# Gates beside the attention heads, branch projections over all heads behind them

## The chip, the cores and the metric

The kernel runs on one core of a Trainium2 chip. The metric is the device time of one execution in microseconds (us). Engines are named as in the profile: PE is TensorE (PEld its weight loads), DVE is VectorE, ACT is ScalarE, POOL is GpSimd, SP is SyncE. SP and POOL issue the DMA transfers that matter here. A name such as L290 is line 290 of the kernel before.

## The reference

One layer of an encoder block: 512 tokens and 16 learned meta tokens (L = 528), model width 1024, float32. Cut to what matters:

```python
xn = rmsnorm(h, norm_mix_g)
proj = xn @ w_in                      # q, k, v of 8 stick-breaking and 8 differential heads
o_sb = stick_breaking(...)            # 528 x 1024, 8 heads of 128
o_df = rmsnorm_per_head(diff_attn(...)) * (1 - lam_init)
y_sb = o_sb @ w_br_sb
y_df = o_df @ w_br_df
gates = sigmoid(xn @ w_gate + b_gate)     # two gates of width 1024
merged = gates[0] * y_sb + gates[1] * y_df
h = h + merged @ w_out
h = h + (silu(hn @ w_ffn_gate) * (hn @ w_ffn_up)) @ w_ffn_down     # hn = rmsnorm(h)
y = rmsnorm(h, norm_final_g)              # meta tokens dropped
```

## The kernel before

**Arithmetic.** Every matrix product is taken in three passes: an operand is split into a high part rounded to the matmul's format (`_h`) and a low rest (`_l`), and PE adds high·high, high·low and low·high in PSUM (`mm3`, L290 to L292). A weight tile is loaded by SP to `wst`, cast to `wh` by ACT (L78), and its rest `wl` is made by DVE (L79).

**Layout.** Activations lie transposed, channels on the 128 partitions and tokens along the line. `xT_h` and `xT_l` hold the normed input, eight tiles of 128 channels; the 16 meta tokens come first, so that the 512 tokens (`QT`) start 64 bytes into a line. A block of a projection (128 output channels, 512 tokens) is 8 input tiles x 3 passes = 24 matmuls of 128x512 into one of four PSUM banks of the pool `ps_mm`; `halves` gives it as two units of 12.

**Order of the work.** A loop runs over two branches (`br`; 0 stick-breaking, 1 differential) and eight heads each. While head `h` computes its attention (`sb_head` or `df_head`, a generator that yields between its scores, its transposes and its product with the values), the loop pops units from the list `units` between these steps: the q, k and v projections of head `h+1` (`sb_units`, `df_units`), the transposing of its v (`turn`, L532 and L539), and what `more` holds. Each popped unit also lets the background list issue one transfer or so by POOL (`tick`): the block sums of the output and down projections' weights, kept in DRAM and partly accumulated there (`ds`, `os`). A scheduler then sets the order on each engine by dependencies and priorities; PSUM evacuations have raised priority. Weights are prepared in the order of the list `stream`.

**Gates and branch projections before.** `more` holds `y_units`: when two heads are done, their outputs (`o`, a high and a low tile for two heads, in the pool `opool`) are multiplied by the two heads' rows of the branch weight. For each of 8 output tiles that is one group of 6 matmuls, a copy by ACT (L799) and a transfer of 256 KB by POOL to `y_part` in DRAM, accumulating there from the second pair on (L801, L803). Of the 16 gate blocks, two (f = 0) run in the first two stick-breaking heads, four (f = 1, 2) around the last differential head, ten in the merge.

**The last head's norm.** The norm of a differential head runs late, in the next head: `late` holds it, with two matmuls by ones (L772, L773), Ln and Exp on ACT (L774, L775), two DVE steps (L776, L777), and the split into `o_h` (ACT, L778) and `o_l` (DVE, L779). The last head's norm is popped after the loop.

**Merge before.** For each of eight channel tiles f the two y tiles are read back from DRAM (`y_back`, L1070), multiplied with the two gates (L1127, POOL for f < 6, DVE for the rest) and added (L1131); `merge_sums` makes the split operands and block sums for the output projection. The residual tile `hres` (L1138, four transfers of 512 KB by POOL) takes the tag `y_sb` of the pool `xtp`; output projection, feed-forward layer and down projection follow and are not touched.

Of the kernel before, what the change touches and what calls it, by code (L numbers as in the profile page):

```python
# [9 lines left out]
F32 = mybir.dt.float32  # L10
# [6 lines left out]
P = 128  # L17
# [24 lines left out]
def block_kernel(ctx: ExitStack, tc: tile.TileContext, x, meta, norm_mix_g, w_in, w_gate, b_gate,  # L42
# [15 lines left out]
    def mm_tile():  # L58
        return ps_mm.tile([P, 512], F32, tag="mm", name="mm")
# [23 lines left out]
    def cols(key, view, c0):  # L83
        stream.append((key, view, c0, P, 0, KT))

    def rows(key, view, c0, k0):
        stream.append((key, view, c0, 512, k0, k0 + 2))

    for h in range(NH):

        for i in (0, 1, 2) if h < SEVEN else (2, 1, 0):
            cols(("sb", h, i), w_in, i * D + h * P)
        if 0 < h < 3:
            cols(("gate", h - 1, 0), w_gate, (h - 1) * D)
        if h > 2:
            rows(("y_sb", h - 3), w_br_sb, (h + 1) % 2 * 512, (h - 3) // 2 * 2)
    for h in range(NH):
        for i in range(3):
            cols(("df", h, i), w_in, (3 + i) * D + h * P)
        if h < 3:  # L100
            rows(("y_sb", h + 5), w_br_sb, (h + 1) % 2 * 512, (h + 5) // 2 * 2)
        else:
            rows(("y_df", h - 3), w_br_df, (h + 1) % 2 * 512, (h - 3) // 2 * 2)
    rows(("y_df", 5), w_br_df, 512, 4)
    for f in range(1, 3):
        for br in range(2):
            cols(("gate", br, f), w_gate, br * D + f * P)
    for i in range(2):
        rows(("y_df", 6 + i), w_br_df, i * 512, 6)
    for f in range(3, KT):  # L110
        for br in range(2):
            cols(("gate", br, f), w_gate, br * D + f * P)
# [220 lines left out]
    y_count, y_out = [0], []  # L333

    tA = xtp.tile([P, 2, 2, 4, HL], F32R, tag="y_sb", name="tA")
    y_part = {n: [ydram.tile([P, SEQ], F32, name=f"{n}_{f}") for f in range(KT)] for n in ("y_sb", "y_df")}
    mid = ExitStack()
    opool = mid.enter_context(tc.tile_pool(name="opool", bufs=2))

# [271 lines left out]
    def sb_head(h, d, o_h, o_l):  # L611
        qh, ql = d["q"]
        kh, kl = d["k"]
        zA, zB = z_tile(), z_tile()
# [79 lines left out]

    late = []

    def df_head(h, d, o_h, o_l):
# [72 lines left out]
        def norm():  # L770
# [7 lines left out]
            nc.scalar.activation(o_h, of, AF.Copy, scale=g_sub)  # L778
            nc.vector.scalar_tensor_tensor(o_l, of, g_sub, o_h.bitcast(F32), op0=ALU.mult, op1=ALU.subtract)  # L779

        late.append(norm)


    def y_units(name, i, o):

        def unit(fs):
            wh, wl = weights((name, i))
            for f in fs:
                ps = mm_tile()
                cs = slice(f % 4 * P, (f % 4 + 1) * P)  # L790
                mm3(ps, [(wh[:, k, cs], wl[:, k, cs], o[0][:, k], o[1][:, k]) for k in range(2)])
                if y_out:
                    ys = y_out[0][:, y_count[0] % KT]
                elif y_count[0] % 2:
                    ys = ap_.tile([P, SEQ], F32, tag="ys", bufs=2, name="ys")
                else:
                    ys = gate_tile(0)
                y_count[0] += 1
                nc.scalar.copy(ys, ps)  # L799
                if i < 2:  # L800
                    nc.gpsimd.dma_start(y_part[name][f], ys)  # L801
                else:
                    nc.gpsimd.dma_start(y_part[name][f], ys, accum_op=ALU.add)  # L803

        f0 = i % 2 * 4
        return [lambda: unit((f0, f0 + 1)), lambda: unit((f0 + 2, f0 + 3))]

    def gate(br, f, dst, func):
        def evac(ps):
# [1 line left out]

        return halves(("gate", br, f), xT, QT, evac)

    g_part = [ydram.tile([P, SEQ], F32, name=f"g_{br}") for br in range(2)]

    def gate_out(br):
        g = gate_tile(0)
        first, second = gate(br, 0, g, AF.Identity)

        def rest():  # L820
            second()
            nc.gpsimd.dma_start(g_part[br], g)

        return [first, rest]

# [179 lines left out]
    order.close()  # L1005
    units[5]()
    turn()
    todo = []
    for br in range(2):
        name, head = (("y_sb", sb_head), ("y_df", df_head))[br]  # L1010
        if br:
            nc.gpsimd.memset(a_s, 0.0)
            y_out.append(xtp.tile([P, KT, SEQ], F32, tag="y_sb", name="y_out"))
        for h in range(NH):
            if (br, h) == (0, 0):
                tB["t"] = opool.tile([P, 2, 2, 4, HL], F32R, tag="y_df", name="tB", bufs=1)
                sums = sum_units()
            if (br, h) == (0, 4):
                df_constants()
            if h % 2 == 0:  # L1020
                o = [opool.tile([P, 2, SEQ], F32R, tag=t, name=t) for t in ("o_h", "o_l")]
            if h + 1 < NH:
                nd, units, turn = (sb_units, df_units)[br](h + 1)
            elif br == 0:
                nd, units, turn = df_units(0)
            else:
                units, turn = [], None
            more = todo.pop(0) if todo else []
            if br == 0 and h < 2:
                more = gate_out(h)  # L1030
            if turn is None:
                sg0 = [gate_tile(br) for br in range(2)]
                units = more + gate(0, 1, sg0[0], AF.Identity) + gate(1, 1, sg0[1], AF.Identity)
            else:
                units = units + more[0:1] + [turn] + more[1:]
# [3 lines left out]
            for n in head(h, d, o[0][:, h % 2], o[1][:, h % 2]):  # L1039
# [6 lines left out]
            if h % 2:  # L1046
                todo += [y_units(name, h - 1 + i, o) for i in range(2)]
    sg1 = [gate_tile(br) for br in range(2)]
    units = gate(0, 2, sg1[0], AF.Identity) + gate(1, 2, sg1[1], AF.Identity)
    units[0]()  # L1050
    late.pop(0)()
    for u in units[1:]:
        u()
    for units in todo:
        for u in units:
            u()
    for sg in sg0 + sg1:
        nc.scalar.activation(sg, sg, AF.Sigmoid)
    att.close()


# [13 lines left out]
    tp_ctx = ExitStack()
# [35 lines left out]
            else:  # L1111
                last_sums.append(rest)

    merge_order = [1, 2, 0, *range(3, KT)]
    ys = [y_back(f) for f in merge_order[:2]]
    for i, f in enumerate(merge_order):
        sg = (sg0, sg1)[i] if i < 2 else [gate_tile(br) for br in range(2)]
        if i + 2 < KT:
            ys.append(y_back(merge_order[i + 2]))
        for br, y in enumerate(ys[i]):  # L1120
            if f == 0:
                nc.sync.dma_start(sg[br], g_part[br])
                nc.scalar.activation(sg[br], sg[br], AF.Sigmoid)
            elif f > 2:
                for u in gate(br, f, sg[br], AF.Sigmoid):
                    u()
            (nc.gpsimd if f < 6 else nc.vector).tensor_tensor(sg[br], sg[br], y, op=ALU.mult)  # L1127
# [81 lines left out]
    def to_out(t, half, ps, op, last=False):  # L1209
        cs = slice(half * 512, (half + 1) * 512)  # L1210
        with tc.high_priority(offset=EVAC):
            nc.vector.tensor_tensor(hres[:, t, cs], hres[:, t, cs], ps, op=op)  # L1212
        if last:
            sq = mgp.tile([P, 512], F32, tag="y_sb", bufs=2, name="sq")
# [320 lines left out]
```

## Time and profile before

| | |
|---|---|
| median of 3 runs | 955.26 us (954.28 to 955.35) |
| the profiled execution | 955.27 us, span 953.5 us, granted PE clock 0.998 |
| PE busy | 940.6 us, 99% |
| DVE, ACT, POOL busy | 720.8, 592.8, 190.5 us (76, 62, 20%) |
| DMA | 158.42 MB, mean 166 GB/s |
| HBM read, written | 133.64 MB, 50.86 MB |

The span is the time from the first to the last instruction; the execution's own time has some 1.8 us around it. In a row of the timeline stand the start, the duration, engine, line, operation, output<-inputs, and in brackets the idle time before it with what ended it. Matmuls are pipelined: they start 0.227 us apart and take 0.39 us each, so the distance between starts is what counts. Start and input norm take the first 55 us, stick-breaking heads run to about 271, differential heads to 497, the last norm to 509, the merge to 573, the output projection to 616, the feed-forward layer to 841, the down projection to the end.

### The profile page before, as it was taken

How to read it: one execution, taken by the hardware profiler on the slowest of the kernel's cores; microseconds unless marked ns; L12 is line 12 of the kernel's file. 1: busy time of each engine (PE TensorE's matmuls, PEld its weight loads, DVE VectorE, ACT ScalarE, POOL GpSimd, SP SyncE). 2: the span in 40 equal slices, each digit the busy share in tenths (PEclk: the TensorE clock that was granted, in tenths of full speed). 3: DMA queues.
4: the chain of work that ended last, by engine and by line, in shares of the span. 5: the costliest groups of instructions: out<-in, count | busy, mean ns of one | idle time of the engine just before them, and what ended most of it. 6: DMA issues, size and time to landing. Idle time of an engine off the chain costs nothing.

```text
span 953.5 us, 16249 instructions
## 1 busy us (share of the span) xinstructions
PE 940.6 (99%) x6105; PEld 851.1 (89%) x6106; DVE 720.8 (76%) x1336; ACT 592.8 (62%) x1137; POOL 190.5 (20%) x212
## 2 busy tenths in 40 slices
PE   8999999999999999999999999999999999999996
PEld 5988989898999899998987888899999999988886
DVE  7978777765677666876662578899888888989875
ACT  7765676666566666666676356765555555666654
POOL 3200121222133343344513530001000000000013
PEclk9999999999999999999999999999999999999999
DMA  8525678778777879799987865527743343276642
GB/s 246 154 63 149 164 176 204 159 166 228 198 178 174 213 170 185 181 204 180 199 198 168 260 197 170 150 78 171 155 123 111 90 120 103 67 255 203 198 151 89
DMA packets 155824, 158.42 MB, mean 166 GB/s; under 512 B 6465, under 2 KB 117218, under 8 KB 155746
## 3 DMA queue, kind: packets, MB, share of 16 engines
q1 hardware_dynamic: 132690, 101.61, 35.5%
q0 software_dynamic: 22896, 55.72, 28.6%
q8 instruction: 48, 0.79, 0.3%
q14 instruction: 30, 0.25, 0.1%
q10 hardware_dynamic: 160, 0.07, 0.0%
HBM read 133.64 MB, written 50.86 MB: 193 GB/s over the span
## 4 chain that ended last, share of the span: by engine, by line
PE 90%; DVE 6%; ACT 2%; issue 1%; DMA 1%; ACTq 0%; DVEq 0%
PE mm L290 21%; PE mm L291 21%; PE mm L292 21%; PE z L290 6%; PE z L291 6%; PE z L292 6%; PE z L708 1%; PE z L707 1%; DVE wl L79 1%; PE tr L556 1%; PE tr L532 1%; PE z L556 1%; DMA slots<-in_w_ffn_down_dram 1%; PE z L584 1%; DVE hres L1212 1%
## 5 line engine op out<-in xcount | busy, mean ns | idle before, releaser
L290 PE MATMUL mm<-xT_h,wh 128*128 128x264 f32 (+2 forms) x656 | 214.5, 327 | 0.5 <-ACT xT_h L912 0.5
L291 PE MATMUL mm<-xT_l,wh 128*128 128x264 f32 (+2 forms) x656 | 213.4, 325 | 0.5
L292 PE MATMUL mm<-xT_h,wl 128*128 128x264 f32 (+2 forms) x656 | 212.5, 324 | 0.0
L79 DVE TENSOR_TENSOR wl<-wst,wh 128x1024 fp32r<-128x1024 f32 (+1 forms) x147 | 164.2, 1120 | 44.9 <-ACT wh L78 44.7
L78 ACT CAST wh<-wst 128x1024 fp32r<-128x1024 f32 (+1 forms) x147 | 141.6, 965 | 84.7 <-PE mm L291 62.5
L291 PEld LDWEIGHTS mm<-xT_l,wh 128*128 128x128 f32 x656 | 123.5, 188 | 10.1 <-DVE xT_l L913 1.3
L290 PEld LDWEIGHTS mm<-xT_h,wh 128*128 128x128 f32 x656 | 123.5, 188 | 10.0 <-ACT xT_h L912 0.9
L292 PEld LDWEIGHTS mm<-xT_h,wl 128*128 128x128 f32 x656 | 123.4, 188 | 10.0
L290 PE MATMUL mm<-hT_h,wh 128*128 128x256 f32 x304 | 85.7, 284 | 0.4 <-ACT hT_h L1169 0.4
L292 PE MATMUL mm<-hT_h,wl 128*128 128x256 f32 x304 | 86.0, 284 | 0.0
L291 PE MATMUL mm<-hT_l,wh 128*128 128x256 f32 x304 | 86.0, 283 | 0.0
L290 PEld LDWEIGHTS mm<-hT_h,wh 128*128 128x128 f32 x304 | 57.3, 189 | 0.6 <-ACT hT_h L1169 0.6
L291 PEld LDWEIGHTS mm<-hT_l,wh 128*128 128x128 f32 x304 | 57.6, 190 | 0.0
L292 PEld LDWEIGHTS mm<-hT_h,wl 128*128 128x128 f32 x304 | 57.4, 189 | 0.0
L711 DVE CUSTOM_DVE_ANT_0 pr<-z,bias 128x144 f32<-128x144 f32 (+3 forms) x64 | 30.9, 501 | 35.0 <-PE z L708 34.9
L290 PE MATMUL mm<-o_h,wh 128*128 128x512 f32 x128 | 53.2, 416 | 0.0
L1437 POOL TENSOR_TENSOR outs<-hres,gF 128x512 f32<-128x512 f32 x4 | 6.2, 1554 | 226.0 <-DVE hres L1423 217.8
L291 PE MATMUL z<-wl,da 128*128 128x512 f32 (+1 forms) x132 | 50.4, 381 | 0.3 <-DVE wl L79 0.3
L145 POOL DMA_DIRECT2D ds<-in_w_ffn_down_dram x36 | 30.1, 840 | 102.3 <-ACT wh L78 68.6
L291 PE MATMUL mm<-o_l,wh 128*128 128x512 f32 x128 | 50.1, 392 | 0.3 <-DVE o_l L779 0.3
L290 PE MATMUL z<-wh,da 128*128 128x512 f32 (+1 forms) x132 | 50.2, 381 | 0.0
L292 PE MATMUL z<-wh,da 128*128 128x512 f32 (+1 forms) x132 | 50.2, 380 | 0.0
(375 smaller groups left out, 2554.4 us busy)
## 6 DMA issues: line engine op xcount, KB each, us to landing
wst<-in_w_in_dram SPq DMA_DIRECT2D x40, 512.0 KB, 5.7
ds<-in_w_ffn_down_dram POOLq DMA_DIRECT2D x30, 512.0 KB, 6.2
wst<-in_w_ffn_gate_dram SPq DMA_DIRECT2D x22, 512.0 KB, 4.0
wsu<-in_w_ffn_up_dram SPq DMA_DIRECT2D x20, 512.0 KB, 3.8
wst<-in_w_gate_dram SPq DMA_DIRECT2D x16, 512.0 KB, 6.8
y_df<-y_out POOLq DMA_DIRECT2D x32, 256.0 KB, 7.4
slots<-ds SPq DMA_DIRECT2D x13, 512.0 KB, 3.4
os<-in_w_out_dram POOLq DMA_DIRECT2D x12, 512.0 KB, 5.4
```

Of the source, the lines that this page charges most:

```text
L78: cast["last"] = (hi_copy or nc.scalar.copy)(hi, src)
L79: (lo_eng or nc.vector).tensor_tensor(lo, src, hi.bitcast(F32), op=ALU.subtract)
L145: tc.add_manual_dep(nc.gpsimd.dma_start(dst, src, **kw).ins, cast["last"].ins.name, paced)
L290: nc.tensor.matmul(ps, lhsT=ah, rhs=bh, start=(start and i == 0), stop=False, skip_group_check=skip)
L291: nc.tensor.matmul(ps, lhsT=ah, rhs=bl, start=False, stop=False, skip_group_check=skip)
L292: nc.tensor.matmul(ps, lhsT=al, rhs=bh, start=False, stop=(stop and i == n - 1), skip_group_check=skip)
L532: nc.tensor.transpose(pt[:, j * P:(j + 1) * P], vT[:, j * P:(j + 1) * P], ident)
L556: nc.tensor.transpose(pt[:, (t - j) * P:(t - j + 1) * P], blocks(t, j * P, (j + 1) * P), ident)
L584: nc.tensor.matmul(ps.rearrange("p (t q) -> p t q", q=P)[:, :, lo_rows:P], lhsT=vf[:, 1], rhs=a_s[:, 0:4 * qn], start=False, stop=True)
L707: nc.tensor.matmul(o, lhsT=q[c][:, qs], rhs=k[c][:, 0, k0:k1], start=True, stop=False)
L708: nc.tensor.matmul(o, lhsT=q[c][:, qs], rhs=k[c][:, 1, k0:k1], start=False, stop=True)
L711: nc.vector.tensor_tensor_reduce(po, zz, bb, scale=1.0, scalar=-3.0e38, op0=ALU.add, op1=ALU.max, accum_out=mx[:, t, c:c + 1])
```

## The change

Gates move ahead: 16 gate blocks run beside the heads, two in stick-breaking heads 0 and 7, one in every other up to differential head 5. ACT adds the bias only, POOL writes each of them to its own tile `g_part` in DRAM (256 KB), and the merge reads it back (`gate_back`, SP) and takes the sigmoid in place.

Branch projections move behind: `branch` is a block of 24 matmuls over all eight heads, in two halves of four heads. The first halves of y_sb 0 and 1 run in differential head 6; their second halves and y_sb 2 and 3 in differential head 7, and ACT copies them to tiles `ys`. y_df 0 to 7 and y_sb 4 to 7 run in the merge, and DVE multiplies them by the gate straight out of PSUM. POOL multiplies the four early ones.

Head outputs are kept: `keep` writes a pair's high and low tile to DRAM (POOL, 512 KB each; four stick-breaking pairs and two differential ones), and `back` reads two pairs by SP into a tile of `xtp` whose data start 64 bytes into the line: stick-breaking heads 0 to 3 under the tag `y_sb` at differential head 4, stick-breaking heads 4 to 7 and differential heads 0 to 3 in place of `xT_h` and `xT_l` at differential head 7. The outputs of differential heads 4 to 7 stay in `opool`, unshifted.

```diff
+    gates = [(br, f) for f in range(KT) for br in range(2)]
...
-            rows(("y_sb", h - 3), w_br_sb, (h + 1) % 2 * 512, (h - 3) // 2 * 2)
+        for _ in range((0, 2)[h] if h < 2 else 1):
+            gate_cols()
...
+    for f in range(4):
+        cols(("y_sb", f), w_br_sb, f * P)
+    for f in range(KT):
+        if f > 3:
+            cols(("y_sb", f), w_br_sb, f * P)
+        cols(("y_df", f), w_br_df, f * P)
...
+        if h % 2:
+            keep(0, h // 2, o)
...
-    def y_units(name, i, o):
-
-        def unit(fs):
-            wh, wl = weights((name, i))
-            for f in fs:
-                ps = mm_tile()
-                cs = slice(f % 4 * P, (f % 4 + 1) * P)
-                mm3(ps, [(wh[:, k, cs], wl[:, k, cs], o[0][:, k], o[1][:, k]) for k in range(2)])
...
-                nc.scalar.copy(ys, ps)
-                if i < 2:
-                    nc.gpsimd.dma_start(y_part[name][f], ys)
-                else:
-                    nc.gpsimd.dma_start(y_part[name][f], ys, accum_op=ALU.add)
...
+    def keep(br, p, o):
+        for i in range(2):
+            nc.gpsimd.dma_start(o_part[br, p][:, i], o[i].bitcast(F32))
...
+    def branch(name, f, evac):
+        cell, key = {}, (name, f)
+
+        def part(k0):
+            if k0 == 0:
+                cell["ps"] = mm_tile()
+            wh, wl = weights(key)
+            mm3(cell["ps"], [(wh[:, k], wl[:, k], *head_out[name, k]) for k in range(k0, k0 + 4)], k0 == 0, k0 == 4)
+
+        def second():
+            part(4)
+            with tc.high_priority(offset=EVAC):
+                evac(cell["ps"])
+
+        return [lambda: part(0), second]
...
+    def back(tile, br, p0):
+        for p in range(p0, p0 + 2):
+            for i in range(2):
+                nc.sync.dma_start(tile[:, p - p0, i].bitcast(F32), o_part[br, p][:, i])
+            for j in range(2):
+                head_out[("y_sb", "y_df")[br], 2 * p + j] = tile[:, p - p0, 0, j], tile[:, p - p0, 1, j]
+
+    def heads_tile(tag):
+        return xtp.tile([P, NM + KT * SEQ], F32R, tag=tag, name="ob")[:, NM:].rearrange("p (a i j c) -> p a i j c", a=2, i=2, j=2)
...
+            if (br, h) == (1, NH - 2):
+                ys = [gate_tile(f % 2) for f in range(4)]
+                early = [branch("y_sb", f, lambda ps, f=f: nc.scalar.copy(ys[f], ps)) for f in range(4)]
+                units = units + [early[0][0], turn, early[1][0]]
+            elif turn is None:
+                back(heads_tile("xT_h"), 0, 2)
+                back(heads_tile("xT_l"), 1, 0)
+                units = [early[0][1], early[1][1], *early[2], *early[3]]
...
+            if (br, h) == (1, 4):
+                back(heads_tile("y_sb"), 0, 0)
...
+            if br and h > 3:
+                head_out["y_df", h] = o[0][:, h % 2], o[1][:, h % 2]
...
+    def gate_back(br, f):
+        g = gate_tile(f % 2) if br == 0 and f > 3 else mgp.tile([P, SEQ], F32, tag="y_df", name="gb", bufs=2)
+        nc.sync.dma_start(g, g_part[br, f])
+        return g
...
+        g = gb[i]
+        nc.scalar.activation(g, g, AF.Sigmoid)
...
+        if br == 0 and f < 4:
+            nc.gpsimd.tensor_tensor(ys[f], g, ys[f], op=ALU.mult)
+            continue
+        later[f] = lambda ps: nc.vector.tensor_tensor(g, ps, g, op=ALU.mult)
+        for u in ahead[f][1:] if f < 2 else branch(("y_sb", "y_df")[br], f, later[f]):
+            u()
```

Three places show how instructions move. A row has its number, the line, the operation and output<-inputs with its shape. First PE in a differential head, where v of the next head is transposed (`vT`, `v_s`) ahead of the product of the attention weights (`a_h`, `a_l`) with the values. Before:

```order
2740 L571 MATMUL tr<-ident,pr 112x64
2741 L532 MATMUL tr<-ident,vT 128x128 x4
2742 L539 MATMUL tr<-ident,v_s 128x128
2743 L290 MATMUL z<-a_h,vh 128x512
2744 L291 MATMUL z<-a_l,vh 128x512
2745 L292 MATMUL z<-a_h,vl 128x512
```

After:

```order
2788 L571 MATMUL tr<-ident,pr 112x64
2789 L532 MATMUL tr<-ident,vT 128x128 x4
2790 L290 MATMUL z<-a_h,vh 128x512
2791 L539 MATMUL tr<-ident,v_s 128x128
2792 L291 MATMUL z<-a_l,vh 128x512
2793 L292 MATMUL z<-a_h,vl 128x512
```

The transpose of `v_s` has moved behind the first matmul of the product.

Second ACT around the last head's norm (`of`, `sq`, `o_h`). Before:

```order
575 L78 CAST sqh<-sq 128x512
576 L774 ACT_TABLE_LOAD
577 L774 ACTIVATE sq<-tr,eps_c 128x512
578 L78 CAST wh<-wst 128x1024
579 L810 ACTIVATE sg<-mm,pcol 128x512
580 L775 ACT_TABLE_LOAD
581 L775 ACTIVATE sq<-sq 128x512
582 L1058 ACT_TABLE_LOAD
583 L1058 ACTIVATE sg<-sg 128x512
584 L778 ACTIVATE o_h<-of,g_sub 128x512
585 L78 CAST wh<-wst 128x1024
```

After:

```order
541 L78 CAST sqh<-sq 128x512
542 L776 ACTIVATE sq<-tr,eps_c 128x512
543 L777 ACTIVATE sq<-sq 128x512
544 L780 ACTIVATE o_h<-of,g_sub 128x512
545 L78 CAST wh<-wst 128x1024
546 L1126 ACT_TABLE_LOAD
547 L1126 ACTIVATE gb<-gb 128x512 x2
```

The gate's evacuation and sigmoid, a weight cast and three table loads have left the chain; one table load stands behind it.

Third SP's queue from the last weights of the heads' projections on (`op` are the kept head outputs in DRAM, branch and pair; `ob` the tiles they are read into). Before:

```order
46 L204 DMA wst<-in_w_in_dram 128x8x128 x3
47 L204 DMA wst<-in_w_br_df_dram 128x2x512 x2
48 L204 DMA wst<-in_w_gate_dram 128x8x128 x4
49 L204 DMA wst<-in_w_br_df_dram 128x2x512 x2
50 L204 DMA wst<-in_w_gate_dram 128x8x128
```

After:

```order
50 L204 DMA wst<-in_w_in_dram 128x8x128 x3
51 L204 DMA wst<-in_w_br_sb_dram 128x8x128 x4
52 L204 DMA wst<-in_w_br_df_dram 128x8x128 x2
53 L1014 DMA ob<-op_0_134 128x1024
54 L1014 DMA ob<-op_2_132 128x1024 x2
55 L1014 DMA ob<-op_3_133 128x1024 x2
56 L1014 DMA ob<-op_0_134 128x1024
57 L1014 DMA ob<-op_1_135 128x1024 x2
58 L204 DMA wst<-in_w_br_df_dram 128x8x128 x2
```

Eight reads of 512 KB now stand between the weights of y_df 1 and y_df 2. The first of them is a differential pair's high tile, the next four are stick-breaking heads 4 to 7.

More of the change, by code (lines that the diff above doesn't have):

```diff
@@ L87, in rows, with gate_cols @@
         stream.append((key, view, c0, 512, k0, k0 + 2))
+    gates = [(br, f) for f in range(KT) for br in range(2)]
+    gate_of = iter(gates)
+    def gate_cols():
+        br, f = next(gate_of)
+        cols(("gate", br, f), w_gate, br * D + f * P)
     for h in range(NH):
@@ L99, in block_kernel @@
             cols(("df", h, i), w_in, (3 + i) * D + h * P)
-        if h < 3:
-            rows(("y_sb", h + 5), w_br_sb, (h + 1) % 2 * 512, (h + 5) // 2 * 2)
-        else:
[L103 to L112, printed above, removed]
+        for _ in range((h < NH - 1) + (h == 0)):
+            gate_cols()
+    for f in range(4):
[4 more added lines that the diff above has]
+        cols(("y_df", f), w_br_df, f * P)
     sums_dram = ctx.enter_context(tc.tile_pool(name="sums_dram", bufs=1, space=bass.MemoryType.DRAM))
@@ L332, in block_kernel @@
     ydram = ctx.enter_context(tc.tile_pool(name="ydram", bufs=1, space=bass.MemoryType.DRAM))
-    y_count, y_out = [0], []
     tA = xtp.tile([P, 2, 2, 4, HL], F32R, tag="y_sb", name="tA")
-    y_part = {n: [ydram.tile([P, SEQ], F32, name=f"{n}_{f}") for f in range(KT)] for n in ("y_sb", "y_df")}
+    g_part = {g: ydram.tile([P, SEQ], F32, name=f"g{g[0]}_{g[1]}") for g in gates}
+    o_part = {(br, p): ydram.tile([P, 2, 2, SEQ], F32, name=f"op{br}_{p}") for br in range(2) for p in range(4 - 2 * br)}
     mid = ExitStack()
@@ L609, in sb_units, with sb_head @@
         return d, q + kv if h < SEVEN else kv[0:3] + q + kv[3:], turn
-    def sb_head(h, d, o_h, o_l):
+    def sb_head(h, d, o_h, o_l, o):
         qh, ql = d["q"]
@@ L695, in block_kernel, with df_head @@
     late = []
-    def df_head(h, d, o_h, o_l):
+    def df_head(h, d, o_h, o_l, o):
         q, k = d["q"], d["k"]
@@ L812, in gate, with gate_out @@
         return halves(("gate", br, f), xT, QT, evac)
-    g_part = [ydram.tile([P, SEQ], F32, name=f"g_{br}") for br in range(2)]
-    def gate_out(br):
+    def gate_out(br, f):
         g = gate_tile(0)
-        first, second = gate(br, 0, g, AF.Identity)
+        first, second = gate(br, f, g, AF.Identity)
         def rest():
             second()
-            nc.gpsimd.dma_start(g_part[br], g)
+            nc.gpsimd.dma_start(g_part[br, f], g)
         return [first, rest]
@@ L1007, in block_kernel @@
     turn()
-    todo = []
+    gate_of = iter(gates)
+    def back(tile, br, p0):
[6 more added lines that the diff above has]
+        return xtp.tile([P, NM + KT * SEQ], F32R, tag=tag, name="ob")[:, NM:].rearrange("p (a i j c) -> p a i j c", a=2, i=2, j=2)
     for br in range(2):
-        name, head = (("y_sb", sb_head), ("y_df", df_head))[br]
+        head = (sb_head, df_head)[br]
         if br:
             nc.gpsimd.memset(a_s, 0.0)
-            y_out.append(xtp.tile([P, KT, SEQ], F32, tag="y_sb", name="y_out"))
         for h in range(NH):
@@ L1027, in block_kernel @@
                 units, turn = [], None
[L1028 to L1033, printed above, removed]
+            if (br, h) == (1, NH - 2):
[6 more added lines that the diff above has]
+                units = [early[0][1], early[1][1], *early[2], *early[3]]
             else:
+                more = [u for _ in range(2 if (br, h) in ((0, 0), (0, NH - 1)) else 1) for u in gate_out(*next(gate_of))]
                 units = units + more[0:1] + [turn] + more[1:]
+            if (br, h) == (1, 4):
+                back(heads_tile("y_sb"), 0, 0)
             if (br, h) == (0, 0):
@@ L1045, in block_kernel @@
             d = nd
[L1046 to L1050, printed above, removed]
-    late.pop(0)()
[L1052 to L1058, printed above, removed]
+            if br and h > 3:
+                head_out["y_df", h] = o[0][:, h % 2], o[1][:, h % 2]
+    later = {}
+    ahead = [branch("y_df", f, lambda ps, f=f: later[f](ps)) for f in range(2)]
+    ahead[0][0]()
+    late.pop(0)()
+    ahead[1][0]()
     att.close()
@@ L1213, in to_out @@
         if last:
-            sq = mgp.tile([P, 512], F32, tag="y_sb", bufs=2, name="sq")
+            sq = mgp.tile([P, 512], F32, tag="y_df", bufs=2, name="sq")
             s0, s1 = ssq[t][:, 0:1], ssq[t][:, 1:2]
```

52 lines of the change are left out of this document (15 added, 37 removed).

## The prediction

> **What bounds the kernel now.** I read the page first, for which engine is full, then the waits of TensorE (PE), then the stretches of the span one by one, and last single rows at the places that the change touches. The page:
>
> ```profile
> span 953.5 us, 16249 instructions
> PE 940.6 (99%) x6105; PEld 851.1 (89%) x6106; DVE 720.8 (76%) x1336; ACT 592.8 (62%) x1137; POOL 190.5 (20%) x212
> ...
> PE 90%; DVE 6%; ACT 2%; issue 1%; DMA 1%; ACTq 0%; DVEq 0%
> ```
>
> PE is busy for 99% of the span and carries 90% of the chain that ended last. The waits of PE (engine, line, what it waited for; total us, times, longest) name what little is missing, and the stretches say where it lies (each engine's busy us and instructions, then clock, DMA share, GB/s):
>
> ```profile
> PE z L556 <- DVE a_l L559: 0.7, 1, 0.7
> ...
> 271.00:497.00 226.00, 226.00 (x1464) 205.42 (x1464) 156.35 (x403) 149.81 (x351) 86.97 (x95) 1.00 0.85 190
> 497.00:510.00 13.00, 12.66 (x54) 9.71 (x53) 5.93 (x7) 10.79 (x14) 0.00 (x0) 1.00 0.26 65
> 510.00:573.00 63.00, 63.00 (x280) 52.14 (x279) 33.87 (x51) 28.41 (x48) 27.95 (x24) 1.00 0.81 233
> ```
>
> The three stretches are the differential heads, the last head's norm and the merge. PE is busy in all of the first and the last, and short of 0.34 us in the norm, at a granted clock of 1.00. A busy PE could still be a slow one, so I took its pace from starts inside one block:
>
> ```profile
> 499.61 0.39 PE L290 MATMUL mm<-xT_h,wh 128*128 128x512 f32 x1
> ...
> 506.88 0.39 PE L292 MATMUL mm<-xT_h,wl 128*128 128x512 f32 x1
> ```
>
> There are 33 starts from the first to the last of these, so 32 steps in 7.27 us: 0.227 us for one. A block of 24 takes 5.45 us, a half block 2.73. The change keeps the matmuls that are not transposes: 16 gate blocks of 24 stay 16, and 64 branch groups of 6 become 16 blocks of 24, 384 either way. What it can win is therefore PE's overhead and stalls, and what it can lose is a new wait of PE.
>
> **The change part by part.** First what it lifts off the other engines, by the longest group of its kind:
>
> ```profile
> L799 ACT COPY y_out<-mm x40: 558/585/588, 284.2 to 519.7; 128x512 f32<-128x512 f32 x40
> ```
>
> The 64 copies out of PSUM (0.58 us each, 37 us of ACT) and their 64 transfers of 256 KB on POOL's queue go, and the 16 reads back; 16 gate writes (2 before), 16 gate reads, 12 writes and 12 reads of 512 KB for the head outputs come. But PE is busy for 226.00 of 226.00 in the differential heads: an ACT with less to do there (149.81 busy) ends nothing earlier. Worth 0; the cover is PE's own work, and it stays.
>
> *More switches.* In the differential heads the transpose of v_s (L539) leaves its place behind the four of L532 and lands behind the first matmul of the attention product. Such a transpose between matmuls is shown in the first head:
>
> ```profile
> 36.55 0.37 PE L290 MATMUL z<-kh,qh 128*128 128x264 f32 x1
> 36.75 0.28 PE L539 MATMUL tr<-ident,v_s 128*128 128x128 f32 x1
> 36.78 0.37 PE L291 MATMUL z<-kl,qh 128*128 128x264 f32 x1
> 36.99 0.28 PE L292 MATMUL z<-kh,ql 128*128 128x264 f32 x1
> ...
> 436.35 0.66 PE L532 MATMUL tr<-ident,vT 128*128 128x128 f32 x4
> 436.84 0.27 PE L539 MATMUL tr<-ident,v_s 128*128 128x128 f32 x1
> 436.87 0.48 PE L290 MATMUL z<-a_h,vh 128*128 128x512 f32 x1
> 437.19 0.39 PE L291 MATMUL z<-a_l,vh 128*128 128x512 f32 x1
> ```
>
> A step of these 264-column matmuls is 0.12 by the pace (0.227 x 264/512). The transpose makes two steps of 0.23 and 0.21, so it costs 0.20; in a row of transposes it costs 0.12 (0.49 for four). And after a row the first matmul takes 0.32 (436.87 to 437.19) where the pace is 0.23: the switch is 0.09. Once more in 7 heads (their v is turned in differential heads 0 to 6) is +0.6 us. Bounds: 0 if the row's end becomes cheaper by as much, +0.7 at 0.10.
>
> *The last norm.* Before, sigmoids of gates stand among its Ln and Exp on ACT, and each change of function loads a table:
>
> ```profile
> 499.37 0.40 PE L773 MATMUL tr<-sqh,ones_r 128*128 128x512 f32 x1
> ...
> 507.83 0.50 PE L290 MATMUL mm<-o_h,wh 128*128 128x512 f32 x1
> 508.62 0.50 PE L291 MATMUL mm<-o_l,wh 128*128 128x512 f32 x1 [0.29 <-DVE o_l L779]
> ...
> 503.30 1.28 ACT L775 ACT_TABLE_LOAD   x1
> 504.59 0.63 ACT L775 ACTIVATE sq<-sq 128x512 f32<-128x512 f32 x1
> ...
> 505.26 0.75 DVE L776 SCALAR_TENSOR_TENSOR sq<-tr,var_max,sq 128x512 f32<-128x512 f32 x1 [1.30 <-ACT sq L775]
> 506.04 0.69 DVE L777 TENSOR_TENSOR of<-of,sq 128x512 f32<-128x512 f32 x1
> ...
> 507.07 0.71 ACT L778 ACTIVATE o_h<-of,g_sub 128x512 fp32r<-128x512 f32 x1
> ...
> 507.81 0.75 DVE L779 SCALAR_TENSOR_TENSOR o_l<-of,g_sub,o_h 128x512 fp32r<-128x512 f32 x1 [1.08 <-ACT o_h L778]
> ```
>
> PE takes 0.79 from 507.83 to 508.62, a stall of 0.56. In the new order no table load and no cast stand inside the chain. An undisturbed norm, of an earlier head, shows its first steps:
>
> ```profile
> 415.83 0.39 PE L773 MATMUL tr<-sqh,ones_r 128*128 128x512 f32 x1
> ...
> 417.04 0.63 ACT L775 ACTIVATE sq<-sq 128x512 f32<-128x512 f32 x1
> ```
>
> From L773's start Exp starts at 1.21; then by the rows above +0.67 to L776, +0.78 to L777, +0.74 to o_h (L777's 0.69 and a hand-over of 0.05), +0.74 to o_l, +0.81 to PE: o_l can be used at 4.95, o_h at 4.2. In the new order 18 matmuls stand between the norm and the first that reads o_h, 20 before o_l: 0.24 + 20 x 0.227 = 4.8. The stall is 0.15, so -0.4 us. Bounds: -0.56 and +0.6, if the chain meets one ACT or DVE instruction of a block's preparation (a cast, about 1.0).
>
> *Head outputs read back.* This is the new wait. The last differential head reads its branch operands from tiles that lie where xT lay. SP may issue the 4 MB only when PE has read xT for the last time, in the head before, at about 462 on the old clock. By the new order and the pace, PE wants the fourth pair of stick-breaking heads, 2.6 MB into the queue, about 12.2 us later. Rows that bear on it:
>
> ```profile
> wst<-os SPq DMA_DIRECT2D x4, 512.0 KB, 3.3
> ...
> hres<-in_x_dram POOLq DMA_DIRECT2D x4, 512.0 KB, 7.6
> ...
> 462.00:480.00 18.00, 18.00 (x101) 15.44 (x100) 10.53 (x33) 13.40 (x33) 10.04 (x11) 1.00 1.02 198
> ...
> 545.00:549.00 4.00, 4.00 (x19) 3.30 (x19) 2.49 (x5) 2.35 (x4) 0.00 (x0) 1.00 1.03 394
> ```
>
> At the 394 GB/s of the last row, with 2.0 us ahead of the first data (3.3 less 512 KB at that rate), the 2.6 MB are in after 2.0 + 6.7 = 8.7 us: no stall. In the stretch itself the DMA engines were full (1.02) at 198 GB/s: 2.0 + 13.2 = 15.2, a stall of 3.0. Much of what filled them was the accumulating of branch products, which goes; the accumulating of the down projection's sums stays. I take 0.5 of the 0 to 3.0, nearer the lower end, since the new reads are plain rows of 4 KB, as the residual's four loads (hres) are, which were in flight at 545. The weights queued behind them (y_df 2 and 3) are cast some 8 us after the 4 MB are through; 0.
>
> Beside it a rule, weighed: the Trainium skill's page "DMA: Bandwidth & Descriptors" (Specifications) gives about 358 GB/s as the limit of HBM for one core. The 394 of the row above is beyond it, so the measurement decides. An estimate by the page: 2.62 MB in 7.3 us, no stall, and the sum lower by 0.5.
>
> *Merge.* The products move to DVE, out of PSUM, and gates come from memory:
>
> ```profile
> sg<-g SPq DMA_DIRECT2D x2, 256.0 KB, 5.1
> ...
> 506.54 0.63 ACT L1058 ACTIVATE sg<-sg 128x512 f32<-128x512 f32 x1
> ...
> L1127 DVE TENSOR_TENSOR sg<-sg,y_df x2: 681/682/684, 569.6 to 576.5; 128x512 f32<-128x512 f32 x2
> ```
>
> One gate buffer's round is a load of 5.1, sigmoid 0.63, product 0.68, sum 0.68 and some 0.3 of hand-overs: 7.4 us, where PE needs 5.45 for each of the first four channel tiles and 10.9 after. The lag grows by 2 us in each of three rounds, 6 us; four PSUM banks let PE go on for three more blocks, 16.4 us. So 0, and up to +0.7 with a late residual tile: it loads behind the first half of y_sb 7, 8.2 us before PE is done, is first wanted about 2.7 us after that, and took 7.6; PE has s1·t1 as cover, and I put 0.1.
>
> *Operands.* Of the 384 branch matmuls 288 now read tiles that start 64 bytes into their line, as those of xT do; 96 (differential heads 4 to 7) and all before read tiles that do not. Groups by shape (count, busy us, mean ns):
>
> ```profile
> L290 PE MATMUL mm<-xT_h,wh 128*128 128x512 f32 x248 | 97.6, 393 | 0.0
> ...
> L291 PE MATMUL mm<-xT_l,wh 128*128 128x512 f32 x248 | 96.8, 390 | 0.0
> L290 PE MATMUL mm<-o_h,wh 128*128 128x512 f32 x128 | 53.2, 416 | 0.0
> L291 PE MATMUL mm<-o_l,wh 128*128 128x512 f32 x128 | 50.1, 392 | 0.3 <-DVE o_l L779 0.3
> ```
>
> The second matmul of a triple takes 392 unshifted and 390 shifted. At most 288 x 2 ns = 0.6; as the rows round and their ends are modelled, half: -0.3.
>
> *Start.* One gate block more stands ahead of the first head's transposes, which wait 0.7 (L556 above), but DVE prepares another tile ahead of a_l. 0, between -0.7 and +0.7.
>
> Sum: +0.6 - 0.4 + 0.5 + 0.1 - 0.3 = +0.5 us. The profiled execution took 955.27 us (span 953.5 and 1.8 around it), the median is 955.26, so one base serves: 955.8 us.
>
> **Rivals.** *Late head outputs (slower).* PE stalls for the full 3.0 instead of 0.5: 958.3. For it speaks the share of 1.02. The Trainium skill's page "DMA: Bandwidth & Descriptors", section "Issuing engines are not separate DMA queues", says that transfers of all issuing engines interleave on the same 16 DMA engines; by that rule SP's reads are not spared by POOL's copies, and the full share above agrees. *Gate rounds (slower).* If a load takes 10 us instead of 5.1, a round is 12.3, the fourth tile's product ends 20.5 us behind PE, and PE waits 4.1 for its bank: 959.9. It decides from a load of 8.6 on (three rounds of 10.9 are 16.4 late); hres took 7.6 in the same stretch, sg 5.1. *Group starts (faster).* The first matmul of a triple takes 416 on the o tiles and 393 on xT: 23 ns x 128 = 2.9 us. If that is a price of short groups on fresh tiles, blocks of 24 shed it: 955.8 - 0.5 (nothing late) - 2.9 = 952.4. Against it: the groups of 12 stand right behind transposes, and 23 ns in the mean is one switch of 0.09 on every fourth of them, the price that the z matmul at 436.87 pays too. The gates now stand in that place and would pay it. It decides once half of the 2.9 goes. *Nothing of it shows:* the read-back is in time and the switches and the norm cancel, 955.3.
>
> **How the numbers follow.** A measurement of this kernel tells about 0.2%, 1.9 us, from no change. The forecast and the cancelling together (954 to 957.1) have 0.50, late head outputs 0.22 (a fifth of it within 957.2), gate rounds 0.10, group starts 0.18 (a tenth of it within 953.4). So faster 0.16, same 0.56, slower 0.28. The range 953.0 to 959.4 takes in the read-back's whole bound, and leaves some 0.12 below and 0.08 above; the likeliest case alone spans 954.5 to 957.
>
> **What would show it.** In the changed profile: the wait on o_l under 0.3; no table load between Ln and o_h; L539 behind z's first matmul, with the next step at 0.3; PE's busy time in the merge at its full share; and at the last head a matmul that reads ob with a DMA as its releaser, which gives the read-back's size. I am wrong if PE waits on a DMA or a bank for more than 2 us, or if a stretch of heads shortens by more than a microsecond.

## The result and the profile after

The changed kernel takes 962.88 us (median of 4, 961.24 to 963.43), the kernel before beside it 954.95 (954.28 to 955.35). The ratio is 1.008, with an interval of 1.0067 to 1.0092: slower by 7.9 us, and outside the predicted range of 953.0 to 959.4. The profiled execution is the fastest of the four, 961.24, and the only one whose granted clock is 0.998; the others have 0.994 to 0.995. The page of after, the lines that answer to those of before:

```profile
span 959.5 us, 16105 instructions
PE 942.2 (98%) x6106; PEld 851.5 (89%) x6106; DVE 725.3 (76%) x1344; ACT 565.4 (59%) x1084; POOL 140.3 (15%) x166
...
PE 87%; DVE 6%; DMA 3%; ACT 2%; issue 1%; SPq 0%; ACTq 0%; DVEq 0%
```

ACT is busy for 27 us less than before and POOL for 50 us less, PE's own work is nearly the same (942.2 us for 940.6), but DMA has grown from 1% of the chain to 3%. The waits of PE in after (total us, times, longest), and the three stretches of the prediction:

```profile
PE mm L291 <- DMA ob<-op: 2.3, 2, 1.5
...
PE mm L290 <- DMA ob<-op: 1.2, 1, 1.2
PE z L291 <- DVE wl L79: 0.8, 1, 0.8
PE z L556 <- DVE a_l L559: 0.8, 1, 0.8
PE z L290 <- DVE a_l L559: 0.7, 1, 0.7
```

```profile
271.00:497.00 226.00, 222.54 (x1444) 202.36 (x1443) 153.11 (x410) 134.33 (x318) 68.80 (x76) 1.00 0.77 186
497.00:510.00 13.00, 13.00 (x67) 10.71 (x66) 8.32 (x19) 7.59 (x17) 0.00 (x0) 1.00 0.66 202
510.00:573.00 63.00, 62.96 (x280) 51.73 (x279) 43.04 (x69) 33.13 (x58) 7.56 (x8) 1.00 0.52 160
```

The 3.46 us that PE is short of in the differential heads are one place, the last head. PE's rows there, then SP's queue, then the transfers (KB each, median us to landing):

```profile
484.88 0.29 PE L710 MATMUL z<-dqk 128*128 128x272 f32 x1
486.36 0.50 PE L290 MATMUL mm<-ob,wh 128*128 128x512 f32 x1 [1.20 <-DMA ob<-op]
488.34 0.50 PE L291 MATMUL mm<-ob,wh 128*128 128x512 f32 x1 [1.48 <-DMA ob<-op]
...
491.00 0.50 PE L291 MATMUL mm<-ob,wh 128*128 128x512 f32 x1 [0.78 <-DMA ob<-op]
```

```profile
219.39 1.29 SPq L1014 DMA_DIRECT2D ob<-op  x3
224.07 1.51 SPq L204 DMA_DIRECT2D wst<-in_w_in_dram  x2
225.63 3.10 SPq L1014 DMA_DIRECT2D ob<-op  x1
...
474.28 7.62 SPq L1014 DMA_DIRECT2D ob<-op  x8
```

```profile
ob<-op SPq DMA_DIRECT2D x12, 512.0 KB, 13.3
```

The read-back is issued from 474.28 on. PE wants the first of it 10.9 us later, at 485.2, and the fourth tile (the low half of the fourth pair) seven matmuls on, 12.5 us after the issue, where the prediction had about 12.2. The matmul that reads that tile starts at 491.00, after 16.7 us.

The first SP row shows something else: the four reads for heads 0 to 3 belong to differential head 4, at about 390 us, but SP issued them at 219, between the weights of a stick-breaking head, because nothing made them wait. ACT then stands at 230.64 for a weight:

```profile
230.64 1.05 ACT L78 CAST wh<-wst 128x1024 fp32r<-128x1024 f32 x1 [2.14 <-DMA wst<-in_w_in_dram]
```

and the a_l of that head comes late to PE (the 0.7 in the waits).

To put a size to each place I take the start of a PE instruction, subtract the nominal time of the PE work ahead of it in program order (the same durations for every kernel), and compare with before. Growth of that difference from place to place, in us, in one profiled execution each (names of the experiments below):

| kernel | start to 225 us | head at 233 us | up to the last head | last head | its norm | to the end of the feed-forward layer | down projection | sum |
|---|---|---|---|---|---|---|---|---|
| after | +0.4 | +0.9 | -0.1 | +4.5 | -0.5 | -0.1 | +0.7 | +5.9 |
| e2_df_later | +1.1 | +0.3 | -0.1 | +3.9 | -0.5 | 0.0 | -0.8 | +3.9 |
| e3_no_sums | +0.6 | +0.7 | -0.1 | +0.1 | -0.5 | -0.1 | -0.7 | -0.1 |
| e5_back_late | +0.7 | 0.0 | -0.1 | +6.1 | -0.5 | -0.1 | -0.7 | +5.3 |
| e6_back_late_no_sums | +0.4 | 0.0 | -0.1 | 0.0 | -0.5 | +0.2 | -0.4 | -0.5 |
| e9_sums_in_ffn | +1.4 | 0.0 | -0.1 | 0.0 | -0.5 | -0.3 | -0.7 | -0.3 |

The first and the last columns scatter by a microsecond or more between kernels that are alike there; the last head does not.

### The profile page after: what moved, and what is told of

Its sections match the earlier page's. It is cut to its first block, busy times and chain, and to the rows that moved or that the text cites. A ratio compares the mean times of both kernels' runs of the same rounds, so it can differ in the third digit from the quotient of the medians.

```text
span 959.5 us, 16105 instructions
## 1 busy us (share of the span) xinstructions
PE 942.2 (98%) x6106; PEld 851.5 (89%) x6106; DVE 725.3 (76%) x1344; ACT 565.4 (59%) x1084; POOL 140.3 (15%) x166
## 4 chain that ended last, share of the span: by engine, by line
PE 87%; DVE 6%; DMA 3%; ACT 2%; issue 1%; SPq 0%; ACTq 0%; DVEq 0%
PE mm L291 20%; PE mm L290 20%; PE mm L292 20%; PE z L290 6%; PE z L291 6%; PE z L292 6%; DMA ob<-op 1%; PE z L710 1%; PE z L709 1%; DVE wl L79 1%; PE tr L556 1%; PE tr L532 1%; DMA slots<-in_w_ffn_down_dram 1%; DMA wst<-in_w_in_dram 1%; PE z L556 1%
## 5 line engine op out<-in xcount | busy, mean ns | idle before, releaser
L290 PE MATMUL mm<-xT_h,wh 128*128 128x264 f32 (+2 forms) x656 | 217.1, 331 | 0.5 <-ACT xT_h L913 0.5
L292 PE MATMUL mm<-t_h,wl 128*128 128x256 f32 x160 | 45.0, 281 | 0.0
L290 PE MATMUL mm<-t_h,wh 128*128 128x256 f32 x160 | 45.0, 281 | 0.0
L291 PE MATMUL mm<-t_l,wh 128*128 128x256 f32 x160 | 44.9, 281 | 0.0
```

What stands on the lines that cost most here:

```text
L290: nc.tensor.matmul(ps, lhsT=ah, rhs=bh, start=(start and i == 0), stop=False, skip_group_check=skip)
L291: nc.tensor.matmul(ps, lhsT=ah, rhs=bl, start=False, stop=False, skip_group_check=skip)
L292: nc.tensor.matmul(ps, lhsT=al, rhs=bh, start=False, stop=(stop and i == n - 1), skip_group_check=skip)
```

## The experiments

**e1_no_wait: is the wait for the read-back the loss?** Heads 0 to 3, long in place, are read where the early y_sb blocks want heads 4 to 7, so these four blocks leave out heads 4 to 7.

```diff
-  mm3(..., [(..., *head_out[name, k]) for k in range(k0, k0 + 4)], ...)
+  mm3(..., [(..., *head_out[name, k - 4 if key[0] == "y_sb" and f < 4 and k > 3 else k]) ...
```

> The second halves of the four early blocks y_sb 0 to 3 take heads 0 to 3 from the tile that is already there, in place of heads 4 to 7; every transfer stays, so their result is another one. Theory A (the wait for the read-back in the last differential head is the main cost): the 4.5 us that PE loses between its norm matmuls of heads 6 and 7 go, 961.2 of the profiled execution becomes 956.7, and if the lower clock of the other executions (0.994 to 0.995) comes from that stall, the median is 956.7 too. Theory B (the time is lost by traffic or order, the wait is only where it shows): the next wait takes its place and 960 or more stay.

Measured 956.03 (954.27 to 957.29, 11 runs), ratio 1.0011 (1.0003 to 1.002). The wait is worth some 6.6 us of the 7.9 (0.8% less 0.11%).

**e2_df_later: too many reads at once?** The four transfers for differential heads 0 to 3, which nobody wants yet, are issued some 18 us later.

```diff
-  back(heads_tile("xT_l"), 1, 0)
-  units = [early[0][1], early[1][1], *early[2], *early[3]]
+  units = [early[0][1], early[1][1], *early[2],
+           lambda: (early[3][0](), back(heads_tile("xT_l"), 1, 0)), early[3][1]]   # and paced on the last cast
```

> The two differential pairs are read back only when ACT has cast the weights of y_df 0; only 2 of the 4 MB are then ahead of PE's first need. Theory A1 (the read-back delays itself, by its own 4 MB): the first 2 MB land some 4 us earlier, the stall falls from 4.1 to under 1, 957 to 958. Theory A2 (the accumulating sums and the copies of q and k of the next head fill the DMA engines): the stall stays above 3, 960 to 963.

Measured 962.23 (958.97 to 964.01, 6 runs), ratio 1.0074 (1.006 to 1.0088): no better. The wait stays with half the volume:

```profile
PE mm L291 <- DMA ob<-op: 3.0, 2, 2.2
```

The last head still loses 3.9 us where after loses 4.5, so the reads' own number is at most a small part of the delay.

**e3_no_sums: the accumulating sums?** POOL issues no block sum of the down projection's weights in the last two differential heads; they go in the merge.

```diff
-  tick(*RATE[br])
+  if (br, h) < (1, NH - 2):
+      tick(*RATE[br])
...                                   # in the merge
+  if len(background) > 6:
+      background.pop(0)()
```

> The background transfers that accumulate the down projection's sums stop during differential heads 6 and 7 and run in the merge. Theory A1: the read-back gains about one transfer of 512 KB, the stall falls by 0.5 to 1.5 us, 960 to 962. Theory A2: it falls by 3 or more, 957 to 959. If the moved sums disturb the merge, its PE time grows beyond full, and the time is above 963.

Measured 958.55 (954.75 to 959.46, 7 runs), ratio 1.0033 (1.0022 to 1.0045); in its profile the last head loses 0.1 us instead of 4.5. Its profiled execution, 954.75, is its fastest, and what the slower ones lose left no rows; e9, which keeps the sums out of the merge too, has no such gap. The stretches from the issue on (clock, DMA share, GB/s at the end of a row), of after first:

```profile
474.00:478.00 4.00, 4.00 (x26) 3.43 (x24) 2.38 (x3) 2.34 (x5) 0.93 (x1) 1.00 1.06 203
478.00:482.00 4.00, 4.00 (x29) 3.49 (x27) 1.44 (x4) 2.35 (x8) 0.00 (x0) 1.00 1.01 227
482.00:486.00 4.00, 3.16 (x18) 2.59 (x16) 1.19 (x8) 0.88 (x3) 2.35 (x2) 1.00 1.08 302
```

and of e3_no_sums:

```profile
474.00:478.00 4.00, 4.00 (x25) 3.33 (x23) 2.38 (x3) 2.33 (x5) 0.00 (x0) 1.00 1.01 230
478.00:482.00 4.00, 4.00 (x27) 3.60 (x27) 1.43 (x4) 2.43 (x8) 0.00 (x0) 1.00 1.01 367
482.00:486.00 4.00, 4.00 (x23) 3.48 (x22) 1.30 (x9) 0.91 (x2) 2.33 (x2) 1.00 1.02 413
```

The DMA engines are full in both. In the first four us they carry much the same (203 and 230 GB/s); after that they carry 367 and 413 without the sums, and 227 and 302 with them. The transfers in the ten us from 474 on, in after:

```profile
DMA packets 1594, 2.34 MB, mean 234 GB/s; under 512 B 82, under 2 KB 1068, under 8 KB 1594
...
ds<-ds POOLq DMA_DIRECT2D x1, 512.0 KB, 12.9
```

One accumulating sum (ds<-ds) is in flight for 12.9 us, and 1068 of the 1594 packets are under 2 KB. Those are mostly pieces of a weight tile (512 bytes each) that SP issued before the read-back and that came late. This is what was issued between 470 and 473 us, in after:

```profile
dqk<-dqk POOLq DMA_DIRECT2D x2, 264.0 KB, 9.3
ds<-ds POOLq DMA_DIRECT2D x1, 512.0 KB, 7.0
wst<-in_w_br_df_dram SPq DMA_DIRECT2D x1, 512.0 KB, 10.7
```

and in e3_no_sums:

```profile
dqk<-dqk POOLq DMA_DIRECT2D x2, 264.0 KB, 5.7
wst<-in_w_br_df_dram SPq DMA_DIRECT2D x1, 512.0 KB, 5.3
```

The sums therefore delay the reads in two ways: one sum is in flight beside the reads, and earlier sums hold up the weight tile and the copies of q and k (dqk), which then lie among the reads. This run takes both away at once. The Trainium skill's page "DMA: Bandwidth & Descriptors", section "Issuing engines are not separate DMA queues", says that what different engines issue shares the same 16 DMA engines; this run agrees: POOL's sums slowed SP's reads.

**e4_one_gate: two gates in one head?** Another account of the head at 233 us: stick-breaking head 7 carries two gate blocks, so its own weights come late. The second is moved to differential head 0.

```diff
-  for _ in range((h < NH - 1) + (h == 0)):                       # order of the weights
+  for _ in range((h < NH - 1) + (h == 1)):
...
-  more = [... range(2 if (br, h) in ((0, 0), (0, NH - 1)) else 1) ...]
+  more = [... range(2 if (br, h) in ((0, 0), (1, 0)) else 1) ...]
```

> The second gate block of stick-breaking head 7 runs in differential head 0. Theory C (its weights come late in that head, so that ACT and DVE make a_l late and PE waits 0.7 to 0.8): 0.9 us less than the changed kernel, 962.0 in the median, 960.3 at its fastest, and no wait on a_l near 233 us. Rival (the wait comes from the order of DVE there and moves to head 0 with the gate): no change, 962.9.

Measured 961.54 (961.33 to 964.58, 5 runs), ratio 1.0076 (1.0064 to 1.0089). The wait on a_l stays at 0.7, so this account does not hold.

**e5_back_late: the early read-back.** The read-back of heads 0 to 3 has to wait for the last weight cast ahead of differential head 4.

```diff
-  nc.sync.dma_start(tile[:, p - p0, i].bitcast(F32), o_part[br, p][:, i])
+  t = nc.sync.dma_start(tile[:, p - p0, i].bitcast(F32), o_part[br, p][:, i])
+  if (br, p0) == (0, 0):
+      paced = mybir.DependencyInfo(mybir.DependencyClass.Sync, mybir.DependencyReason.DATA)
+      tc.add_manual_dep(t.ins, cast["last"].ins.name, paced)
```

> The read of stick-breaking heads 0 to 3, which SP issues at 219 us among the weights of head 7, waits for a cast of differential head 3, near its place in the program; nothing else changes. Theory D (that early burst of 2 MB makes the weights of stick-breaking heads 7 and 8 late): the wait of z on a_l near 233 us goes, 0.9 us less than the changed kernel in the profile (960.3), and its share of the scatter in the others; the stall of 4 us in the last head stays. Rival (weights are late there for another reason): 961 to 963, the wait stays.

Measured 960.7 (957.86 to 963.09, 6 runs), ratio 1.0068 (1.0053 to 1.0082). The wait at 233 us is gone (0.0 in the table). The last head loses 6.1 us here, more than after, and its rows show why (PE's matmuls, then two stretches, in which the clock stands third from the end):

```profile
486.79 0.49 PE L290 MATMUL mm<-ob,wh 128*128 128x512 f32 x1 [2.18 <-DMA ob<-op]
489.10 0.80 PE L291 MATMUL mm<-ob,wh 128*128 128x512 f32 x1 [1.82 <-DMA ob<-op]
489.69 0.63 PE L292 MATMUL mm<-ob,wl 128*128 128x512 f32 x1
...
492.25 0.47 PE L292 MATMUL mm<-ob,wl 128*128 128x512 f32 x1
```

```profile
488.00:492.00 4.00, 2.90 (x7) 2.27 (x8) 0.50 (x1) 0.00 (x0) 0.00 (x0) 0.62 1.02 413
492.00:496.00 4.00, 4.00 (x19) 3.39 (x18) 1.69 (x3) 2.74 (x4) 0.84 (x1) 0.95 0.84 280
```

After waits of 2.18 and 1.82 with one matmul between them, the granted clock is 0.62 over the 4 us from 488 to 492 (0.50 from 489.1 to 492.3). Six steps from 489.69 to 492.25 take 0.427 each instead of 0.227, which with the first makes about 1.5 us. The profile of e4_one_gate shows the same after waits of 2.00 and 1.43: a clock of 0.50 from 490.0 to 493.3. In the profiled execution of after the waits of 1.20 and 1.48 left the clock at 1.00. The timed runs below a clock of 0.997 all belong to the four kernels with a long wait there (after, e2, e4, e5). That this is also the 1.6 us between after's profiled execution and its median is likely by the clocks of 0.994 and 0.995, and not shown, since those runs left no rows.

**e6_back_late_no_sums: both mended.** The edits of e5 and e3 together.

> Both: the early read held back, and no sums during differential heads 6 and 7. If the two explain the change, the median falls to that of the kernel before within 1 us: 954 to 955.6, and the scatter of the run without sums (954.75 to 959.46) shrinks. If its scatter came from the read-back in the last head in executions that the profile does not show, the median stays near 958.5.

Measured 954.43 (953.03 to 958.42, 11 runs), ratio 1.0007 (0.9996 to 1.0017): level with before, no wait on a DMA.

**e7_back_late_no_wait.** The edits of e5 and e1 together: the sums stay, the wait cannot occur.

> The early read held back, and the second halves of y_sb 0 to 3 take heads 0 to 3 in place of heads 4 to 7 (another result), so that no product of the last head waits for a read. Theory D: 956.0 of the run without the wait falls by about 1, to 955, with no wait on a DMA's weights in stick-breaking head 7. Rival: 956 as before.

Measured 954.9 (954.11 to 955.79, 11 runs), ratio 1.0006 (0.9998 to 1.0015). The same by another way: with the sums in place but no wait on the read-back, nothing is lost, so the sums cost through the read-back alone.

**e8_unshifted: the 64 bytes.** e6 with the read-back tiles starting at a line's beginning.

```diff
-  return xtp.tile([P, NM + KT * SEQ], ...)[:, NM:].rearrange(...)
+  return xtp.tile([P, NM + KT * SEQ], ...)[:, 0:KT * SEQ].rearrange(...)
```

> As the run with both (early read held back, no sums in heads 6 and 7), but the tiles that are read back start at the line's begin, not 64 bytes into it. The prediction's term for the shift was 0.3 us, with 0.6 as its bound: 0.3 more than that run. If the shift is worth nothing, the same time; if a conflict of addresses hides there, more than 1 us.

Measured 959.01 (957.6 to 960.43, 5 runs), ratio 1.005 (1.0038 to 1.0062). This run mixed two things. The starts of matmuls that read ob are 233.2 ns apart (e6: 227.3), 1.7 us over 288. But its merge also has two waits for a PSUM bank that no other profile has, behind a gate load:

```profile
PE mm L290 <- DVE sg L1138: 1.3, 1, 1.3
PE mm L290 <- DVE gb L1138: 1.3, 1, 1.3
...
ACT gb L1130 <- DMA gb<-g: 19.5, 7, 8.6
```

A gate load cost ACT a wait of 8.6 while the displaced sums ran in the merge. That is the mechanism of the rival "gate rounds". In e6, with the same sums there, the longest such wait is 4.6 and no bank is waited for; why the loads came later here than in e6 is not shown.

**e9_sums_in_ffn.** e5 with the sums left out of the last two heads and of the merge; they go with the ticks of the feed-forward layer.

```diff
-  tick(*RATE[br])
+  if (br, h) < (1, NH - 2):
+      tick(*RATE[br])
```

> The version that puts both found costs right: heads 0-3 are read back behind the weights of differential head 3, and no sum of the down projection's weights is issued in the last two differential heads; the sums left over go with the feed-forward layer's ticks instead of the merge. Theory A (accumulating sums delay the read-back, an early read-back delays one head's weights, nothing else is lost): no DMA wait of PE in the last head, no gate wait in the merge, 954.0 to 954.6, level with before at 954.5, and a narrower scatter than the 953.0 to 958.4 that the same kernel had with the sums in the merge. Rival G (the group starts of my prediction: longer groups shed 2.9 us once the waits are gone): 951.6 or less. Rival S (scatter is of the chip, not of the sums in the merge): again runs above 957.

Measured 954.55 (953.95 to 955.73, 11 runs) beside 954.95 of before, ratio 0.9999 (0.999 to 1.0008). Its longest run is 2.7 us under that of e6, so the sums in the merge were the likely source of that scatter. The ten us from 474 on now carry 3.30 MB instead of 2.34:

```profile
DMA packets 946, 3.30 MB, mean 330 GB/s; under 512 B 117, under 2 KB 152, under 8 KB 945
```

**e10_unshifted_clean.** e9 with the unshifted tiles of e8.

> As e9, but the three tiles of head outputs read back start at a line's beginning instead of 64 bytes into it (same bytes moved, same instructions). The earlier pair with the sums in the merge gave +4.6 us, of which 6 ns x 288 matmuls = 1.7 by the pace (233.2 against 227.3 ns) and 3.0 were bank waits behind late gate loads. Theory O (the pace is the whole of the operands' price, the bank waits came from the sums in the merge): e9 + 1.7, about 956.0, no bank wait in the merge. Rival T (unshifted tiles slow the transfers too, so the bank waits come back): e9 + 3 or more.

Measured 956.17 (955.45 to 957.64, 11 runs), ratio 1.0015 (1.0006 to 1.0024): 1.6 us over e9, where the pace alone gives 6.0 ns x 288 = 1.7 (233.2 against 227.2 ns between the starts of successive matmuls that read ob, 268 steps in each). No wait for a bank. The second matmul of a triple, by shape, of e9 and then of e10:

```profile
L291 PE MATMUL mm<-ob,wh 128*128 128x512 f32 x96 | 37.4, 390 | 0.0
```

```profile
L291 PE MATMUL mm<-ob,wh 128*128 128x512 f32 x96 | 37.8, 394 | 0.0
```

**e11_lam_early.** e9 with the four loads of the lambda vectors issued two heads earlier, into a tile of their own (`df_loads()` at stick-breaking head 2, `df_constants()` left at head 4).

> As e9, but the four loads of the lambda vectors are issued two stick-breaking heads earlier, into a tile of their own. In earlier runs DVE and ACT stood 4.1 to 5.8 us on these loads at the fifth head, and PE waited 0.4 to 1.1 us behind ACT there. Theory L: that wait of PE is gone, 0.4 to 1.1 below e9. Rival M (the wait moves: ACT is late for another reason in that head): same as e9 within 0.3.

Measured 954.29 (953.94 to 955.36, 11 runs), ratio 0.9998 (0.9989 to 1.0007); 0.26 below e9 is within the scatter. The wait of PE behind ACT there (0.5 in e9) is gone, and another stands one head ahead, since ACT now meets the same chain earlier (at 142.39 it has stood 2.89 us for DVE's part of it):

```profile
146.04 0.44 PE L556 MATMUL z<-ident,s 128*128 128x128 f32 x2 [0.84 <-DVE a_l L559]
```

## Why the prediction was wrong, by its own steps

- **Head outputs read back: the step that failed.** I took 0.5 of 0 to 3.0; it is 4.5 in the profiled execution, and by e1 the wait is 6.6 of the medians' 7.9. That PE would want the last tile after 12.2 us was about right (12.5); the arrival was put between 8.7 and 15.2 and was 16.7. The slow end divided 2.6 MB by 198 GB/s, the whole traffic of a full stretch, as if the reads had all of it. I noted that the accumulating for the down projection stays, and then gave it no share. I also preferred the fast end because the reads are plain rows of 4 KB; but what else is in flight set the rate. With the sums out of the last two heads the same reads are in time and the last head loses 0.0 to 0.1 (e3, e6, e9), while halving the reads hardly helps (e2). The rival "late head outputs" was the right one, and its price of 958.3 a bound that was none. The sign that the prediction gave for being wrong, a wait of PE on a DMA of more than 2 us, is there: 3.46 us in all.
- **The clock was not in the sum.** I priced the stall at its length. With a long wait PE then also ran at 0.427 a step for a while (e4, e5).
- **The early read-back was not seen.** I followed the queue for the second read-back and not for the first: the code calls it at differential head 4, its tile and its data were free much earlier, and SP took it at 219 us. +0.9 in the profiled execution; e5 removes it.
- **More switches, +0.6: wrong by its whole size, inside its bound of 0.** In before, the transposes at 436.35 (shown there) lead to z's third matmul in 1.07, and in after too (a row of before, then three of after):

```profile
437.42 0.39 PE L292 MATMUL z<-a_h,vl 128*128 128x512 f32 x1
```

```profile
478.47 0.65 PE L532 MATMUL tr<-ident,vT 128*128 128x128 f32 x4
...
479.20 0.27 PE L539 MATMUL tr<-ident,v_s 128*128 128x128 f32 x1
...
479.54 0.39 PE L292 MATMUL z<-a_h,vl 128*128 128x512 f32 x1
```

  The row became cheaper by what the single transpose cost; over the seven heads the difference is -0.1.
- **The last norm, -0.4: right.** Measured -0.5. The chain runs without a table load, and PE takes 0.35 from the second matmul at 520.52 to the next at 520.87, a wait of 0.1 where it was 0.56 (ACT's rows, then PE's):

```profile
517.12 0.63 ACT L777 ACTIVATE sq<-sq 128x512 f32<-128x512 f32 x1
519.30 0.72 ACT L780 ACTIVATE o_h<-of,g_sub 128x512 fp32r<-128x512 f32 x1 [1.55 <-DVE of L779]
...
520.29 0.63 PE L290 MATMUL mm<-o_h,wh 128*128 128x512 f32 x2
520.87 0.50 PE L291 MATMUL mm<-o_l,wh 128*128 128x512 f32 x1
```

- **Merge, 0: right here** (PE busy for 62.96 of 63.00). The condition of "gate rounds" was real, though: e8 met it when the sums ran there.
- **Operands, -0.3: about 0.** The second matmul of a triple takes 390 shifted, against 392 in the o tiles of before. The shift matters in another way than I costed: the read-back tiles without it are 1.6 us slower (e10), while the o tiles, which have none in either run, lose less (227.0 ns a step in e9, 228.9 in e10, 86 steps each). What in the tile's place does that stays open.
- **Group starts (the faster rival): did not happen.** The first matmuls of the gates take the place, as the argument against it had said. In e9, which has no stall:

```profile
L290 PE MATMUL mm<-xT_h,wh 128*128 128x512 f32 x248 | 100.1, 404 | 0.0
...
L290 PE MATMUL mm<-ob,wh 128*128 128x512 f32 x96 | 38.0, 395 | 0.0
...
L290 PE MATMUL mm<-o_h,wh 128*128 128x512 f32 x32 | 12.3, 389 | 0.0
```

  Together 150.4 us; before, 97.6 + 53.2 = 150.8.
- **Start, 0: +0.4**, within its bounds. **Relief of ACT, DVE and the DMA engines, 0: right:** with every wait mended (e6, e9) the kernel is level with before, so the change's own worth is nothing, as PE's 226.00 of 226.00 had said.

## What to carry to other kernels

A new transfer's arrival is not its bytes over the bandwidth of the stretch: list what else is in flight there, above all accumulating transfers, and give the new one only the rest. A transfer that the program may issue early is issued early, so look where its tile and its data come free, and pace it on the work that it belongs to if weights wait behind it. Where one engine is 99% busy, relief of the others was worth nothing here, and a stall can cost more than its length.

## What had not been expected of the hardware

- Two waits of PE of 2.18 and 1.82 us with one matmul between them brought the granted clock to 0.62 over 4 us and the step to 0.427 (e5), and so did 2.00 and 1.43 (e4); waits of 1.20 and 1.48 did not (after). The Trainium skill's page "TensorE: Matmul & The Clock Gate", Part 1, puts the drop at an idle window of about 3.4 us. The rows agree if a single matmul does not count: 4.5 us from the end of the matmul before, at 484.61, to 489.10 in e5, 3.9 us from 486.17 to 490.09 in e4, and 3.2 us from 485.17 to 488.34 in after.
- Full DMA engines carried 203 to 302 GB/s in the first twelve us of the read-back with accumulating transfers and a late weight tile's 512-byte pieces among the packets, and up to 413 without.
- An accumulating sum costs the DMA engines twice what a plain copy does. In the profile of after, the plain copy of 512 KB issued at 192.67 (an early block sum) takes 35.2% of the 16 engines over 192 to 197 us, 1.8 us of all of them, and lands after 3.9; the accumulating one issued at 671.57 takes 60.5% over 672 to 678, 3.6 us, and lands after 5.8. No run put plain copies in the place of the sums, so how much of the delay comes from the accumulating itself is not shown.
- The same matmul ran at 233.2 ns a step from tiles at a line's start (e10) and at 227.2 from the same tiles 64 bytes on (e9).
